# Small transfers on ScalarE's DMA queue, blocks picked by DMA reads, and new ranks in a planned mixing stage

## The chip, the cores and the metric

One Trainium2 chip, one of its cores. The metric is the device time of one execution of the kernel, in microseconds (us); of several runs the median counts. The engines of the core are TensorE (PE, with its weight loads as PEld), VectorE (DVE), ScalarE (ACT), GpSimd (POOL) and SyncE (SP). Each works through its own instructions in order; semaphores tie the engines together. A DMA is issued by an instruction on one engine (here SP, ACT or POOL) and carried out by 16 DMA engines that all issuing engines share.

## The reference

One layer of a trunk block on 1024 tokens of width 1024: RMSNorm, one projection of 9504 columns, two recurrent branches (RWKV-7 and HGRN2), a gated merge, an output projection; then cross-attention into 256 memory tokens, then a SwiGLU FFN. The change touches the RWKV-7 branch, which is, per head of width 64:

```python
def step(state, inp):
    r_t, w_t, k_t, v_t, a_t, b_t = inp
    sa = jnp.einsum('bhvk,bhk->bhv', state, a_t)
    state = (state * w_t[:, :, None, :] + sa[..., None] * b_t[:, :, None, :]
             + v_t[..., None] * k_t[:, :, None, :])
    return state, jnp.einsum('bhvk,bhk->bhv', state, r_t)
_, o = lax.scan(step, s0, (tm(r_h), tm(w_h), tm(k_mod), tm(v_h), tm(-kk), tm(kk * a_h)))
```

The kernel computes this in chunks of 64 tokens: within a chunk the delta rule is a unit triangular 64 x 64 system per head, whose inverse is built from 16 x 16 diagonal blocks, then 32 x 32, then 64 x 64.

## The kernel before

The program has three parts. `rw_prep` projects the RWKV columns and writes the branch's factors to DRAM scratch (`ar_d`, `bk_d`, `v_d`, `z_d`). `mixing` does everything up to the merged activations `y_d`. Then come output projection, attention and FFN, ordered by an automatic scheduler.

In `mixing` the order is written by a planner (`Pace`) while the program is built. Matmuls of the remaining projection (HGRN columns and gates, tile `pproj`, 768 slots of three 128x512 matmuls) are the filling; all other work is a set of generators that yield requests `on(engine, tiles, prio=...)`. `note` gives each recorded operation a planned start and duration; a request is due when its inputs, its buffer and its conditions are ready on that planned clock, and among due requests of an engine the one with the smallest `due + 2 * prio` is recorded next. PE records one such group, then three projection slots, and so on. The result is one fixed order per engine: where a transfer or an engine is later than planned, the engine waits at that instruction, with everything behind it.

RWKV work is 16 jobs (`job(n)`, 128 tokens of four pairs of heads each, so eight 64 x 64 systems for each half of the partitions). A job runs:

- SP loads AR and BK; PE forms the scores `psc`, which are masked into AR, SR and BS (BS holds the triangular systems, 64 columns each).
- The 16 x 16 diagonal blocks of BS are copied into BP by four `copy_predicated` on DVE with the mask `pk`; SP writes BP to scratch `Ad`, and SP reads `Ad` twice into Aq, so that each partition holds one 16 x 16 block.
- DVE inverts all blocks by back substitution: nine steps of a product (`pr`) and a sum (into Tq), with POOL setting the diagonal of Aq in between.
- SP writes Tq to scratch `Td` and reads it back as T1 (shown as T in the profile).
- PE, DVE and ACT grow the inverse to 32 x 32 and 64 x 64 (`py1`, `pu1`, `py2`, `pu2` in the code, py and pu in the profile; results in Yd, UD, TT, U, Y).
- The two chunks are scanned in order: `cm`, `po` matmuls with the state Z, copies R and Z by ACT, decay by DVE. Job n's scan needs job n-1's.
- Group norm and the merge terms follow on DVE, ACT and POOL (st, xc, zb), and SP writes the result to `ya_d`.

After every fourth job the results of half the tokens are complete: `merge(j, h)` reads ya_d, the spilled gates sa_d and sb_d, PE transposes (`pya`), DVE and POOL multiply and add, SP writes `y_d`. For the last column block `last_gates` does it with tiles kept on chip. The HGRN branch (`hgrn`, `state`, `level`, `blocks`; tiles poh, pyb, sc, Sh) runs in between, fed by evictions `ev_*` of the projection's PSUM tiles by ACT. At the very end of `mixing` two key tiles of the attention are projected (`pproj<-mT,wkey`, 48 matmuls), after the last transpose `pya`. Attention begins with the values (`pvv`, `values(c)`): its memory tokens mT and weights wraw use SBUF that held the projection's input uh and ul.

The requests that the change ranks anew: DVE's inversion steps (prio 0), the evictions `ev_*` (prio -1).

Of the kernel before, what the change touches and what calls it, by code (L numbers as in the profile page):

```python
# [10 lines left out]
F32 = mybir.dt.float32  # L11
F32R = mybir.dt.float32r
AF = mybir.ActivationFunctionType
# [5 lines left out]
P = 128  # L19
# [13 lines left out]
class Pace:  # L33
# [82 lines left out]
    def note(self, e, op, a, kw):  # L116
# [68 lines left out]
def tile_trunk(ctx, tc, x, mem, norm_mix_g, w_in, rw_mu, rw_w0, rw_w2, rw_a0, rw_a2, rw_g2,  # L185
# [523 lines left out]
    def unit_blocks(pk, hm, lo16, Yd):  # L709
# [3 lines left out]
        f = Yd.rearrange("p e t -> p (e t)")  # L713

        nc.gpsimd.memset(f[:, 0:64], 1.0)
        f3 = f[:, 0:64].rearrange("p (m t) -> p m t", t=16)
        for b in (0, 64):
            r = f3[b:b + 64]

            sel(out=r, in_=r, compare_op=ALU.is_gt, fill=0.0, base=0, pattern=[[16, 4], [1, 16]], channel_multiplier=-1)  # L720
            sel(out=r, in_=r, compare_op=ALU.is_ge, fill=0.0, base=0, pattern=[[-16, 4], [0, 16]], channel_multiplier=1)
        nc.gpsimd.tensor_copy(pk, f3)
# [14 lines left out]
    def mixing(mctx):  # L737
# [28 lines left out]
        pk = cp.tile([P, 4, 16], U8, name="pk")  # L766
# [3 lines left out]
        BP = cp.tile([P, 8, 16], F32, name="BP")  # L770
        Yd = cp.tile([P, 8, 32], F32, name="Yd")
        nc.gpsimd.memset(BP, 0.0)
        unit_blocks(pk, hm, lo16, Yd)
# [82 lines left out]

        def job(n):
# [65 lines left out]
            for ms in ((7, 6), (5, 4), (3, 2), (1, 0)):  # L923
                yield on("DVE", Aq, Tq)
# [9 lines left out]
            yield on("SP", Tq, prio=-1)  # L934
            Td = pace.scratch(dram, [P, 8, 16], tag="Td", bufs=2)
            nc.sync.dma_start(out=Td.rearrange("(r i g) e t -> g e r i t", r=8, g=2).rearrange("g e r i t -> (g e) (r i) t"),
                              in_=Tq.rearrange("p i t -> p (i t)"))
            yield on("SP", Td, prio=-1, room=((fp, "T1", 1),), cond=lambda: n < 1 or ("U32", n - 1) in flags)
            T1 = fp.tile([P, 8, 16], F32, tag="T1", name="T1")
            nc.sync.dma_start(out=T1, in_=Td)  # L940
# [251 lines left out]
        def ev_k(j, h, ps):  # L1192
            yield on("ACT", ps, func=AF.Sigmoid, prio=-1, cond=lambda: j == 0 or ("free", j - 1, h) in flags)
# [8 lines left out]
        def ev_q(j, h, ps):  # L1202
            yield on("ACT", ps, func=AF.Sigmoid, prio=-1, room=room("td"), cond=lambda: j == 0 or ("free", j - 1, h) in flags)
            t = TD("sgq")
            act(t, ps, AF.Sigmoid)
            yield on("DVE", t, prio=-1)
# [958 lines left out]
    n = 0  # L2165
# [181 lines left out]
```

## Time and profile before

| | us |
|---|---|
| median of 3 runs | 2354.96 (2354.55 to 2357.52) |
| profiled execution | 2350.59 |
| its span | 2348.9 |
| PE busy in the span | 2260.1 (96%) |
| DVE, ACT, POOL busy | 1578.6 (67%), 1129.5 (48%), 1028.3 (44%) |

The 1.7 us between the span and the execution's own time lie around the first and the last instruction. Matmuls are pipelined, so a busy PE is not PE at its peak; the bare time between the starts of two matmuls says more. `mixing` runs on PE from about 400 us to 1333.8 us of the span. In the profile nearly all of its instructions carry line 103, where the planner's wrapper issues them; they are told apart by tile names.

### The profile page before, as it was taken

Reading aid. Unit: us, or ns where it says so; the run is one execution under the profiler, and the core shown is the slowest. Engines: PE = TensorE matmul, PEld = TensorE weight load, DVE = VectorE, ACT = ScalarE, POOL = GpSimd, SP = SyncE. Lnnn points to the kernel's source line nnn. Section 1 sums busy time; section 2 is a strip of 40 time slices with the busy share of each in tenths; the row PEclk is TensorE's granted clock in tenths of the full one; section 3 lists DMA queues with packets and bytes.
Section 4 is the critical chain, followed back from the end, with each engine's and each line's share of the span. In section 5 each row is a group of like instructions: output and inputs, shape, how many; then the busy total and the mean of one; then the engine's idle time right before and its main releaser. Section 6 shows DMA issues by size and latency. Waiting matters only on the chain.

```text
span 2348.9 us, 46523 instructions
## 1 busy us (share of the span) xinstructions
PE 2260.1 (96%) x18006; PEld 1845.8 (79%) x18006; DVE 1578.6 (67%) x2585; ACT 1129.5 (48%) x2199; POOL 1028.3 (44%) x1100
## 2 busy tenths in 40 slices
PE   7999999999999999999997499999999999999998
PEld 5788887787888787777876488888888888888887
DVE  5888884767677777767775365655768765656665
ACT  6545554655655555456555232543453233334543
POOL 3655546656566564554653200000266565552212
PEclk9999999999999999999998699999999999999999
DMA  5444445342444343433423797225944334248653
GB/s 171 127 135 121 131 125 150 80 117 48 110 100 123 75 126 114 115 88 84 128 70 95 237 353 267 73 60 207 282 162 132 110 96 130 82 152 299 220 170 118
DMA packets 393690, 327.92 MB, mean 140 GB/s; under 512 B 107595, under 2 KB 318653, under 8 KB 392061
## 3 DMA queue, kind: packets, MB, share of 16 engines
q1 hardware_dynamic: 391549, 319.17, 45.2%
q0 software_dynamic: 1344, 4.72, 0.5%
q8 instruction: 142, 2.33, 0.4%
q10 hardware_dynamic: 576, 1.05, 0.1%
q14 instruction: 79, 0.65, 0.1%
HBM read 228.12 MB, written 96.21 MB: 138 GB/s over the span
## 4 chain that ended last, share of the span: by engine, by line
PE 73%; DVE 5%; DMA 3%; ACT 2%; issue 1%; POOL 1%; SPq 0%; POOLq 0%; DVEq 0%; ACTq 0%
PE pproj L103 21%; PE P L301 6%; PE P L302 6%; PE P L300 6%; PE acc L301 3%; PE acc L300 3%; PE acc L302 3%; PE pw L302 2%; PE pw L300 2%; PE pw L301 2%; PE cm L103 2%; PE po L103 1%; PE psc L103 1%; PE poh L103 1%; PE pq L302 1%; PE pq L301 1%
## 5 line engine op out<-in xcount | busy, mean ns | idle before, releaser
L103 PE MATMUL pproj<-uh,whi 128*128 128x512 f32 x768 | 319.4, 416 | 4.9 <-DVE q L103 4.9
L103 PE MATMUL pproj<-uh,wlo 128*128 128x512 f32 x768 | 301.1, 392 | 1.7 <-POOL wlo L103 1.7
L103 PE MATMUL pproj<-ul,whi 128*128 128x512 f32 x768 | 301.3, 392 | 0.0
L286 POOL TENSOR_TENSOR wl<-wraw,wh 128x512 fp32r<-128x512 f32 x87 | 121.9, 1408 | 200.7 <-ACT wh L282 167.7
L282 ACT ACTIVATE whi<-wraw 128x512 fp32r<-128x512 f32 (+1 forms) x166 | 100.4, 617 | 195.3 <-PE pw L302 76.6
L103 POOL TENSOR_TENSOR wlo<-wraw,whi 128x512 fp32r<-128x512 f32 x96 | 132.4, 1391 | 137.1 <-ACT whi L103 103.4
L300 PE MATMUL pproj<-uh,whi 128*128 128x512 f32 (+1 forms) x432 | 176.8, 410 | 0.9 <-ACT uh L328 0.7
L103 PEld LDWEIGHTS pproj<-uh,whi 128*128 128x128 f32 x768 | 144.3, 188 | 40.0 <-DVE q L103 6.0
L302 PE MATMUL pproj<-uh,wlo 128*128 128x512 f32 (+1 forms) x432 | 169.9, 393 | 1.8 <-POOL wlo L286 1.8
L103 PEld LDWEIGHTS pproj<-ul,whi 128*128 128x128 f32 x768 | 144.6, 188 | 32.2
L301 PE MATMUL pproj<-ul,whi 128*128 128x512 f32 (+1 forms) x432 | 169.8, 393 | 0.0
L103 PEld LDWEIGHTS pproj<-uh,wlo 128*128 128x128 f32 x768 | 145.0, 189 | 27.0 <-POOL wlo L103 2.1
L277 POOL TENSOR_TENSOR ss<-ss,nhalf 128x4 f32<-128x4 f32 (+1 forms) x7 | 6.2, 884 | 328.9 <-DMA wraw<-in_xa_wo_dram 186.6
L286 DVE TENSOR_TENSOR wlo<-wraw,whi 128x512 fp32r<-128x512 f32 x134 | 92.4, 698 | 74.6 <-ACT whi L282 72.7
L103 ACT ACT_TABLE_LOAD x100 | 128.3, 1283 | 23.1 <-PE pproj L103 11.4
L286 POOL TENSOR_TENSOR wlT<-wraw,whT 128x512 fp32r<-128x512 f32 x72 | 102.2, 1427 | 83.2 <-ACT whT L282 72.8
L282 ACT ACTIVATE wh<-wraw 128x512 fp32r<-128x512 f32 x143 | 87.1, 624 | 93.2 <-PE P L301 66.8
L301 PE MATMUL acc<-wl,th 128*128 128x512 f32 x308 | 119.9, 389 | 0.0
L300 PE MATMUL acc<-wh,th 128*128 128x512 f32 x308 | 119.8, 389 | 0.0
L302 PE MATMUL acc<-wh,tl 128*128 128x512 f32 x308 | 119.8, 389 | 0.0
L2291 DVE TENSOR_TENSOR tl<-tl,th 128x512 fp32r<-128x512 f32 x77 | 60.7, 801 | 61.1 <-ACT th L2290 60.3
L302 PE MATMUL pw<-whi,al 128*128 128x512 f32 x256 | 100.1, 391 | 1.2 <-DVE al L286 1.2
(460 smaller groups left out, 6322.1 us busy)
## 6 DMA issues: line engine op xcount, KB each, us to landing
wraw<-in_w_in_dram SPq DMA_DIRECT2D x148, 256.0 KB
wraw<-in_ffn_w_dram SPq DMA_DIRECT2D x145, 256.0 KB
y<-in_ffn_w_dram SPq DMA_DIRECT2D x22, 512.0 KB
wsum_d<-y SPq DMA_DIRECT2D x11, 1024.0 KB
hsum_d<-s SPq DMA_DIRECT2D x44, 256.0 KB
tl<-hsum_d SPq DMA_DIRECT2D x44, 256.0 KB
wraw<-wsum_d SPq DMA_DIRECT2D x44, 256.0 KB
hid_d<-s SPq DMA_DIRECT2D x33, 256.0 KB
```

The source lines that it names most:

```text
L103: r = getattr(self.engine, op)(*a, **kw)
L277: nc.gpsimd.tensor_tensor(dst, tmp, nhalf[:, 0:n], op=ALU.pow)
L282: nc.scalar.activation(hi, src, AF.Copy)
L286: e.tensor_tensor(lo, src, hi.bitcast(F32), op=ALU.subtract)
L300: nc.tensor.matmul(ps, ah, bh, start=first, stop=False)
L301: nc.tensor.matmul(ps, ah, bl, start=False, stop=False)
L302: nc.tensor.matmul(ps, al, bh, start=False, stop=last)
L2291: tt(hl, hl.bitcast(F32), hh.bitcast(F32), op=ALU.subtract)
```

## The change

Four edits, all in `mixing` and its planner:

- The six transfers of a job around the inversion (one write, two reads of Ad, Td, T1) are issued by ACT instead of SP; the write of Ad is now two DMAs, one for each half of the partitions.
- BP, `pk` and the four predicated copies are gone. The whole of BS goes to DRAM (64 columns per row instead of 16), and the two reads of Aq pick the diagonal blocks, 16 runs of 16 floats for each of 64 partitions, by an access pattern with a pitch of 16 x 64 + 16. Since what is below and on the blocks' diagonals now arrives too, DVE multiplies Aq by a mask `tri` once per job.
- Ranks: the inversion's DVE steps go from prio 0 to -1, the projection's evictions from -1 to -2.
- The planner takes an ACT transfer to be independent of SP's queue, and to land 2.0 us plus its bytes by rate after its start.

```diff
         if op == "dma_start":
-            start = max(start, self.landings[-8], self.read.get(aps[0].name, 0.0))
+            start = max(start, self.landings[-8] if e == "SP" else 0.0, self.read.get(aps[0].name, 0.0))
...
-            took = 0.5
-            self.dma = max(start + 0.9, self.dma) + 4 * math.prod(aps[0].shape) / rate
-            self.landings.append(self.dma + 1.1)
-            late = self.landings[-1] - start - took
+            took = 0.62
+            if e == "ACT":
+                late = 2.0 + 4 * math.prod(aps[0].shape) / rate - took
+            else:
+                self.dma = max(start + 0.9, self.dma) + 4 * math.prod(aps[0].shape) / rate
+                self.landings.append(self.dma + 1.1)
+                late = self.landings[-1] - start - took
...
-    def unit_blocks(pk, hm, lo16, Yd):
+    def unit_blocks(tri, hm, lo16, Yd):
...
+        nc.gpsimd.memset(tri, 1.0)
+        sel(out=tri, in_=tri, compare_op=ALU.is_gt, fill=0.0, base=0, pattern=[[-1, 16], [1, 16]], channel_multiplier=0)
...
+        DIAG = 16 * 64 + 16
+        def blocks16(d):
+            rows = d.rearrange("e h (b y) -> (e h b) y", y=DIAG)[:, 0:16 * 64]
+            return rows.rearrange("r (s t) -> r s t", t=64)[:, :, 0:16]
...
-            yield on("DVE", BS, over=(BP,), cond=lambda: n < 1 or ("Ad", n - 1) in flags)
-            for b in range(4):
-                nc.vector.copy_predicated(BP, pk[:, b, :].unsqueeze(1).to_broadcast([P, 8, 16]),
-                                          BS[:, :, 16 * b:16 * b + 16])
-            Ad = pace.scratch(dram, [64, 16, 16], tag="Ad", bufs=2)
-            yield on("SP", BP, prio=-1)
-            nc.sync.dma_start(out=Ad.rearrange("(e r) s t -> (r s) e t", r=8), in_=BP)
+            yield on("ACT", BS, prio=-1)
+            Ad = pace.scratch(dram, [8, 2, 4 * DIAG], tag="Ad", bufs=2)
+            for hh in range(2):
+                nc.scalar.dma_start(out=Ad[:, hh, 0:64 * 64].rearrange("e (s t) -> s e t", t=64), in_=BS[H[hh]])
...
-            yield on("SP", Ad, prio=-1, room=((fp, "Aq", 1), (fp, "Tq", 1)), cond=lambda: n < 1 or ("inv", n - 1) in flags)
+            yield on("ACT", Ad, prio=-1, room=((fp, "Aq", 1), (fp, "Tq", 1)), cond=lambda: n < 1 or ("inv", n - 1) in flags)
...
-                nc.sync.dma_start(out=Aq[64 * g:64 * g + 64], in_=Ad)
+                nc.scalar.dma_start(out=Aq[64 * g:64 * g + 64], in_=blocks16(Ad))
...
-            yield on("DVE", Aq, Tq)
+            yield on("DVE", Aq, Tq, prio=-1)
...
+            nc.vector.tensor_tensor(Aq, Aq, tri, op=ALU.mult)
...
-                yield on("DVE", Aq, Tq)
+                yield on("DVE", Aq, Tq, prio=-1)
...
-            yield on("SP", Tq, prio=-1)
+            yield on("ACT", Tq, prio=-1)
...
-            nc.sync.dma_start(out=T1, in_=Td)
+            nc.scalar.dma_start(out=T1, in_=Td)
...
-            yield on("ACT", ps, func=AF.Sigmoid, prio=-1, cond=lambda: j == 0 or ("free", j - 1, h) in flags)
+            yield on("ACT", ps, func=AF.Sigmoid, prio=-2, cond=lambda: j == 0 or ("free", j - 1, h) in flags)
```

The last pair stands for all evictions (`ev_k`, `ev_q`, `ev_s`, `ev_g`, `ev`, `ev_sa`), on DVE too.

Since the planner decides the order, the program's order shows what moves. Before `mixing` nothing does, on any engine, and PE's instructions behind `mixing` stand as before. First place, PE at the end of `mixing`. Before, behind the last projection matmul (which stands just ahead of these rows) come job 15's two scan steps (cm, po), the end of the HGRN branch (psA to poh, pyb), five transposes and the keys:

```order
L103 MATMUL cm<-Z,AR_3701 64x64 x8
L103 MATMUL po<-Z,AR_3701 64x64 x8
L103 MATMUL psA<-m_15512 32x32 x8
L103 MATMUL psl<-m_15534 64x64 x8
L103 MATMUL poh<-iv,sc 64x128 x8
L103 MATMUL poh<-Sh,qe 64x128 x8
L103 MATMUL cm<-R,U 64x64 x8
L103 MATMUL cm<-Z,BKT 64x64 x8
L103 MATMUL po<-Z,SR 64x64 x8
L103 MATMUL cm<-Z,AR_3701 64x64 x8
L103 MATMUL po<-Z,AR_3701 64x64 x8
L103 MATMUL cm<-R,U 64x64 x8
```

Now PE has only this behind its last projection matmuls (first row), up to the first value matmul of the attention:

```order
L103 MATMUL pproj<-ul,whi 128x512
L103 MATMUL pya<-ident,mya 128x128 x4
L103 MATMUL pproj<-mT,wkey 128x256 x48
L303 MATMUL pvv<-whi,mT 128x512
L304 MATMUL pvv<-wlo,mT 128x512
```

Everything else has moved ahead of the last projection matmul. Second place, PE where job 15's last scan matmul (po<-Z,SR) now stands:

```order
L103 MATMUL pproj<-ul,whi 128x512
L103 MATMUL po<-Z,SR 64x64 x8
L103 MATMUL poh<-iv,sc 64x128 x8
L103 MATMUL poh<-Sh,qe 64x128 x8
L103 MATMUL pproj<-uh,whi 128x512
L103 MATMUL pproj<-uh,wlo 128x512
```

Behind it stand 246 projection matmuls, where there were none before. Counted in projection slots, a job's way from its last score to its py1 falls from 52 to 38 on average over the 16 jobs. Third place, ACT around job 15's Td, which SP issued before:

```order
L103 ACTIVATE sgs<-pproj 128x512
L103 ACTIVATE whi<-wraw 128x512
L103 ACTIVATE sgg<-pproj 128x512
L103 ACTIVATE Y<-py_14268 32x256
L103 DMA Td<-Tq 16x64x16
L103 ACTIVATE U<-pu_14303 32x8x32 x2
L103 ACTIVATE R<-cm 128x256
L103 DMA T_14370<-Td 128x128
L103 ACTIVATE Z<-cm 64x4x64 x2
```

The transfers of job 15 now stand among job 14's scan copies (R, Z), evictions (sgs, sgg) and weight splits (whi).

More of the change, by code (lines that the diff above doesn't have):

```diff
@@ L763, in mixing @@
             nc.gpsimd.memset(U[64 * hh + 32:64 * hh + 64, :, 0:32], 0.0)
-        pk = cp.tile([P, 4, 16], U8, name="pk")
+        tri = cp.tile([P, 16, 16], F32, name="tri")
         hm = cp.tile([P, 2, 16], F32, name="hm")
         lo16 = cp.tile([P, 16], U8, name="lo16")
-        BP = cp.tile([P, 8, 16], F32, name="BP")
         Yd = cp.tile([P, 8, 32], F32, name="Yd")
-        nc.gpsimd.memset(BP, 0.0)
-        unit_blocks(pk, hm, lo16, Yd)
+        unit_blocks(tri, hm, lo16, Yd)
         cm = pc.tile([P, 2, 4, 64], F32, name="cm")
@@ L1202, in ev_q @@
         def ev_q(j, h, ps):
-            yield on("ACT", ps, func=AF.Sigmoid, prio=-1, room=room("td"), cond=lambda: j == 0 or ("free", j - 1, h) in flags)
+            yield on("ACT", ps, func=AF.Sigmoid, prio=-2, room=room("td"), cond=lambda: j == 0 or ("free", j - 1, h) in flags)
             t = TD("sgq")
             act(t, ps, AF.Sigmoid)
-            yield on("DVE", t, prio=-1)
+            yield on("DVE", t, prio=-2)
             q = X[j]["q", h] = B2("q")
@@ L1212, in ev_s @@
         def ev_s(j, h, ps):
-            yield on("ACT", ps, func=AF.Sigmoid, prio=-1, room=room("td"), cond=lambda: j == 0 or ("out", j - 1, h) in flags)
+            yield on("ACT", ps, func=AF.Sigmoid, prio=-2, room=room("td"), cond=lambda: j == 0 or ("out", j - 1, h) in flags)
             t = TD("sgs")
             act(t, ps, AF.Sigmoid)
-            yield on("DVE", t, prio=-1)
+            yield on("DVE", t, prio=-2)
             s = X[j]["sb", h] = pace.hold(B2("sb"))
@@ L1221, in ev_g @@
         def ev_g(j, h, ps):
-            yield on("ACT", ps, func=AF.Sigmoid, prio=-1, room=room("td"))
+            yield on("ACT", ps, func=AF.Sigmoid, prio=-2, room=room("td"))
             t, s = TD("sgg"), X[j]["sb", h]
@@ L1232, in f @@
             def f(j, h, ps):
-                yield on("ACT", ps, prio=-1, room=room("td"))
+                yield on("ACT", ps, prio=-2, room=room("td"))
                 t = X[j][name, h] = TD(name)
@@ L1270, in ev_sa @@
             if j == NU - 1:
-                yield on("ACT", ps, func=AF.Sigmoid, prio=-1, room=room("td"))
+                yield on("ACT", ps, func=AF.Sigmoid, prio=-2, room=room("td"))
                 t = TD("sa")
@@ L1281, in ev_sa @@
             nc.sync.dma_start(out=g, in_=gd[j, h])
-            yield on("ACT", ps, func=AF.Sigmoid, prio=-1)
+            yield on("ACT", ps, func=AF.Sigmoid, prio=-2)
             act(t, ps, AF.Sigmoid)
```

12 lines of the change are left out of this document (2 added, 10 removed).

## The prediction

> **What bounds the kernel now.** I read the page's busy shares first, then the 40 slices, then the windows of the stages, then PE's timeline in the one stage that stands out.
>
> ```profile
> span 2348.9 us, 46523 instructions
> PE 2260.1 (96%) x18006; PEld 1845.8 (79%) x18006; DVE 1578.6 (67%) x2585; ACT 1129.5 (48%) x2199; POOL 1028.3 (44%) x1100
> PE   7999999999999999999997499999999999999998
> PEclk9999999999999999999998699999999999999999
> ```
>
> PE is busy nearly throughout, so a faster DVE or a shorter transfer is worth nothing unless PE waits for it. The slices show one hole, the 22nd and 23rd (7, then 4), and there the granted clock falls too (8, 6). In numbers, each window's columns being its length, busy us of PE, PEld, DVE, ACT, POOL, then PE's clock, DMA share and GB/s:
>
> ```profile
> 400.00:1267.50 867.50, 850.57 (x11316) 684.01 (x11315) 623.59 (x1278) 494.17 (x1070) 497.23 (x544) 1.00 0.37 94
> 1267.50:1333.80 66.30, 24.30 (x282) 21.41 (x282) 17.95 (x31) 14.06 (x42) 17.16 (x16) 0.61 0.69 225
> 1333.80:1465.00 131.20, 127.42 (x628) 107.57 (x627) 75.15 (x121) 44.72 (x80) 2.10 (x3) 1.00 0.85 301
> ```
>
> The first row is `mixing` up to its last projection matmul: PE idles 17 us in 867. The second is from there to the attention's first value matmul: 66.3 us with 24.3 us of work, most of it at half clock. The hole in PE's own words, start and duration, with the idle time before it in brackets:
>
> ```profile
> 1266.95 0.39 PE L103 MATMUL pproj<-uh,wlo 128*128 128x512 f32 x1
> 1267.18 0.39 PE L103 MATMUL pproj<-ul,whi 128*128 128x512 f32 x1
> 1267.49 0.69 PE L103 MATMUL cm<-Z,AR 128*64 128x64 f32 x16
> 1275.98 1.12 PE L103 MATMUL cm<-Z,AR 128*64 128x64 f32 x16 [1.05 <-DVE Z L103]
> 1285.46 1.52 PE L103 MATMUL po<-Z,SR 128*64 128x64 f32 x16 [4.37 <-ACT Z L103]
> 1306.73 2.83 PE L103 MATMUL pya<-ident,mya 128*128 128x128 f32 x12 [19.75 <-DMA mya<-ya_d]
> 1325.08 1.08 PE L103 MATMUL pya<-ident,mya 128*128 128x128 f32 x4 [6.29 <-DMA mya<-ya_d]
> 1333.76 0.39 PE L300 MATMUL pvv<-whi,mT 128*128 128x512 f32 x1
> ```
>
> The filling has run out at 1267.5, but job 15 has only begun its scan (cm). Its scan, its group norm, its write to ya_d and the merges that read it back are a chain with nothing beside it: its three waits for mya alone are 34.2 us (the group's row stands in the sum below). So the RWKV jobs' latency, harmless while projection matmuls fill in, sets the end of `mixing`.
>
> Why is job 15 late? Its transfers and its inversion:
>
> ```profile
> 1211.89 0.37 SPq L103 DMA_DIRECT2D Ad<-BP  x1
> 1215.30 1.20 SPq L103 DMA_DIRECT2D Aq<-Ad  x2
> 1221.68 0.28 DVE L103 TENSOR_TENSOR pr<-Aq 128x128 f32<-128x128 f32 x1
> 1239.17 0.42 DVE L103 TENSOR_REDUCE Tq<-pr 128x16 f32<-128x256 f32 x1
> 1239.62 0.56 SPq L103 DMA_DIRECT2D Td<-Tq  x1
> 1242.22 0.34 SPq L103 DMA_DIRECT2D T<-Td  x1
> ```
>
> From BP's write to T's read it is 30.3 us, of which 17.9 are the inversion's sixteen DVE products and sums plus its first two steps, with other DVE work placed between them at equal or better rank. The transfers themselves are short: Td landed 2.6 us after its issue.
>
> **The change, part by part.** *The predicated copies go, a mask comes.*
>
> ```profile
> L103 DVE COPY_PREDICATED BP<-pk,BS 128x128 f32<-128x128 uint8 x64 | 45.1, 705 | 1.7
> 1264.59 0.43 DVE L103 TENSOR_TENSOR m<-m,k 128x256 f32<-128x256 f32 x1 [2.39 <-ACT m L103]
> ```
>
> DVE loses 45.1 us and gains 16 products of 128x256, each 0.43 by the row of that shape: 6.9. DVE was busy 623.6 of 867.5 us, so the net 38 us come off an engine that does not bound the stage. Directly they are worth nothing; per job they take some 2.4 us out of the chain.
>
> *The transfers go to ACT.* Six issues per job, 96 in all. Issues of these tiles held SP 0.34 to 0.60 us each; ACT's own first issue in this trace is like that:
>
> ```profile
> 1274.97 0.39 ACTq L1704 DMA_DIRECT2D wraw<-in_xa_wv_dram  x1
> ```
>
> At 0.5 us it is 48 us more on ACT, from 494.2 to 542 of 867.5 us (62%). That is covered as long as ACT is not what PE waits for. Beside the issue there is a wait: ACT stands at Aq's read until Ad has landed, and at T's read until Td has. Ahead of T's read the order has three copies (U twice, R) behind Td's issue, and behind it Z, for which PE waits. So a late landing that SP took at no cost now holds R, Z and the evictions. Per wait between 0 (the planner has put it where it is over) and 2.6 us (the landing row above, nothing between), 32 times: 0 to 83 us of ACT, of which PE sees what its order has no slack for.
>
> *Blocks picked by reads.* Ad's write has 1024 runs as before, of 256 B instead of 64; the reads of Aq have 2048 runs of 64 B instead of 128 of 1 KB. Td's write, 1024 runs of 64 B, is the nearest row. The window in which it ran almost alone:
>
> ```profile
> 1239.60:1242.30 2.70, 2.70 (x25) 1.98 (x23) 1.74 (x5) 2.65 (x5) 1.99 (x3) 1.00 0.23 24
> ```
>
> A share of 0.23 of 16 engines over 2.7 us is 9.9 engine-us, so 9.7 ns a run; 2048 runs are 1.2 us over 16 engines. Bounds for what a job's T loses by it: nothing (the two reads overlap in flight) to 2.6 us (a second Td on top). I take 1.2, less than the 2.4 us that the copies give back.
>
> *Ranks.* Inversion first takes the waiting out of 17.9 us on DVE; evictions first take it out of PE's waits for PSUM. No edit has a price on PE by itself. What counts is the order that comes out: job 15's last scan matmul now has 246 projection matmuls behind it, and only one transpose and the keys stand behind the last of these. At 0.23 us from start to start (1266.95 to 1267.18) the 246 are 57 us of cover. The chain behind that matmul was 1285.46 to 1325.08, 40 us, and had DMA traffic for the attention in its way. It fits.
>
> **The sum**, against the profiled execution's 2350.59 us (1.7 outside the span).
>
> - The stretch 1267.5 to 1333.8 goes: -66.3.
> - Its work stays, at full clock. The groups:
>
> ```profile
> L103 PE MATMUL pproj<-mT,wkey 128*128 128x256 f32 x48 | 8.1, 345 | 0.0
> L103 PE MATMUL pya<-ident,mya 128*128 128x128 f32 x20 | 5.0, 426 | 34.2 <-DMA mya<-ya_d 34.2
> 1243.10 0.66 PE L103 MATMUL pkh<-ident,kh 128*128 128x128 f32 x4
> 1344.80 0.28 PE L301 MATMUL pk<-mT,whi 128*128 128x256 f32 x1
> 1344.92 0.28 PE L302 MATMUL pk<-mT,wlo 128*128 128x256 f32 x1
> ```
>
>   Five transposes at 0.66 (pkh, same shape) are 3.3 instead of 5.0; 48 key matmuls at 0.12 from start to start (pk, same shape) 5.8 instead of 8.1; of the other 11.2 us about half ran slow (cm 1.12 instead of 0.69), which leaves about 8.6. Together +17.7, of which 6.5 (one transpose, keys) stand behind the last projection matmul.
> - Late next is the attention's start, since its weights and mT use SBUF of uh and ul and cannot be loaded while projections read these. Before, the same loads, issued by ACT at 1274.97, became usable here:
>
> ```profile
> 1282.58 0.63 ACT L282 ACTIVATE whi<-wraw 128x512 fp32r<-128x512 f32 x1 [3.70 <-DMA wraw<-in_xa_wv_dram]
> 1283.24 0.69 DVE L286 TENSOR_TENSOR wlo<-wraw,whi 128x512 fp32r<-128x512 f32 x1 [5.22 <-ACT whi L282]
> ```
>
>   That is 9.0 us from the issue to the end of wlo, and the issue comes about 0.5 us after the last projection matmul. So the first value matmul can start 9.5 us after it, of which 6.5 are covered: +3.0 (0 to 8, the upper end if mT, which ended up in the same burst, comes last).
> - Behind that, what the attention had loaded during the hole must be loaded beside its work. It eats a weight tile of 256 KB in six matmuls, 1.4 us or 187 GB/s, and the third window row shows 301 GB/s moved; but other loads share these, and that row lost 3.8 us to waits. I take the like of it once more: +3 (0 to 12).
> - `mixing` itself, whose PE order is now denser: the first window row lost 17 us in 16 jobs. Between -10 (evictions first removes waits for PSUM) and +83 (every landing wait of ACT reaches PE) I stay near that row, a third more: +5.
>
> -66.3 + 17.7 + 3.0 + 3 + 5 = -37.6, or 2313.0 on the profiled execution's level. The median of the runs, 2354.96, lies 4.4 above that execution; on its level **2317 us**. The forecast's own range is 2299 (mixing -10, no gap, no refill loss) to 2331.
>
> **The rivals.** *ACT pays.* If each of the 32 landing waits costs PE 1 us instead of 32 waits costing 5 together, that is +27: 2344. For it: the order has T's read three copies behind Td's issue, 1.1 us of work for a landing of 2.6, at 0.38 for a copy:
>
> ```profile
> 1258.80 0.38 ACT L103 ACTIVATE U<-pu 32x256 f32<-32x256 f32 x1 [0.48 <-DVE U L103]
> ```
>
> Against it: the planner places the read where it expects the landing, and ACT keeps 38% of the stage free.
>
> *PE waits at py1, slower.* PE's order is fixed and py1 now stands 38 slots behind a job's last score instead of 52. A slot is 867.5 / 768 = 1.13 us, so T has to be there 16 us sooner. Sure of that are 2.4 us from the copies and what the rank takes out of the 17.9. If T is late by 4 us in each job, PE waits 64 us instead of 5: 2376. It turns slower than before when the lateness passes (37.6 + 5) / 16 = 2.7 us a job. For it: 2048 short runs per job, and ACT in line for everything. Against it: Td's 2.6 us, and a case where the old queue itself was the delay:
>
> ```profile
> 832.83 0.37 SPq L103 DMA_DIRECT2D Ad<-BP  x1
> 833.29 2.58 SPq L103 DMA_DIRECT2D Z<-v_d  x4
> 835.96 0.55 SPq L103 DMA_DIRECT2D sa_d<-sa  x1
> 836.61 2.56 SPq L103 DMA_DIRECT2D AR<-ar_d  x4
> 839.26 0.56 SPq L103 DMA_DIRECT2D BK<-bk_d  x1
> 839.87 0.51 SPq L103 DMA_DIRECT2D zb<-z_d  x1
> 840.43 1.60 SPq L103 DMA_DIRECT2D Aq<-Ad  x2
> ```
>
> Here 7.6 us passed against 3.4 for job 15, with eleven other transfers issued by SP in between. The Trainium skill, "DMA: Bandwidth & Descriptors", section "Issuing engines are not separate DMA queues", says that DMAs from all issuing engines run on the same 16 DMA engines, so that a second one saves the issuing time alone. By that rule a landing gets no shorter, which is this rival's case; the two rows agree in that the 4.2 us between them are other issues, not a longer landing.
>
> *The attention starves.* Gap 8 and refill 12 instead of 3 and 3: +14, 2331. For it: the DMA share of 0.85 in the third row. The Trainium skill, "TensorE: Matmul & The Clock Gate", part 1, has the clock halve after an idle window of about 3.4 us; by it the gap of 3 costs no clock and one of 8 costs about 2 us more (an estimate from that page). The hole above agrees, with a clock of 0.61.
>
> *The hole stays.* If the merges remain a chain (pya from 1306.73 to 1326.2, 19.5 us) whatever the jobs do, 20 us of the gain are gone: 2337. Against it stand the orders: four of five transposes have moved in front.
>
> **How the numbers follow.** Forecast 0.60, ACT pays 0.17, attention starves 0.11, hole stays 0.04, PE waits at py1 0.08. Measurement tells about 0.2%, 4.7 us, from no change. Only the last case is slower; the upper end of "ACT pays" touches no change, 0.04. Faster 0.88, same 0.04, slower 0.08. The range: 2299 from the forecast's lower end, 2344 as the price of "ACT pays", which leaves out the slower case and the tails.
>
> **What would show it.** Right: the slices lose their hole and half clock; the wait of pya for mya falls from 34.2 us to a few; job 15's last po stands some 60 us or more ahead of the last projection matmul; the window from the last projection matmul to the first pvv is 9 to 15 us instead of 66; from inversion's first to last DVE row under 12 us instead of 17.9; ACT's busy share in `mixing` unchanged (issues aren't counted) but waits for Ad and Td by name. Wrong: PE idle in `mixing` over 45 us, with py waiting for T (PE waits), or cm and py waiting for ACT's Z, R, U (ACT pays); or over 10 us idle in the first 130 us of the attention.

## The result, and the profile after

Four runs of the changed kernel: 2314.25 to 2322.77 us, median **2317.44**; of the kernel before beside them 2353.94 to 2357.52, median 2354.76. The ratio is 0.9842, 95% interval 0.982 to 0.9864: 37 us faster. The profiled execution is the slowest of the four (2322.77, span 2321.1), 5.3 us above the median, where the profiled one of before lay 4.4 below the median that the forecast was set on. So from profile to profile only 27.8 us are gone, and the terms below add up to that.

The page of the changed kernel, span, busy shares and slices:

```profile
span 2321.1 us, 46517 instructions
PE 2266.5 (98%) x18006; PEld 1845.9 (80%) x18006; DVE 1528.3 (66%) x2510; ACT 1134.9 (49%) x2214; POOL 1027.7 (44%) x1109
PE   7999999999999999999999999999999999999998
PEclk9999999999999999999999999999999999999999
```

The hole in the 22nd and 23rd slice is gone, with its half clock. The stages, in windows with the same columns as before (length, busy us of PE, PEld, DVE, ACT, POOL, clock, DMA share, GB/s): `mixing` to the end of its last projection matmul, from there to the first value matmul, the next 131 us, and all that is behind that value matmul:

```profile
400.00:1291.50 891.50, 869.46 (x11560) 697.84 (x11559) 586.56 (x1224) 510.11 (x1120) 513.88 (x567) 0.99 0.42 104
1291.50:1298.96 7.46, 6.46 (x53) 6.21 (x52) 1.73 (x4) 1.23 (x2) 3.15 (x3) 1.00 0.96 316
1298.96:1430.26 131.30, 128.11 (x620) 106.27 (x621) 79.27 (x128) 46.07 (x83) 2.66 (x4) 1.00 0.93 332
1298.96:2321.10 1022.14, 1007.56 (x4644) 834.24 (x4644) 646.70 (x935) 409.39 (x761) 306.39 (x228) 0.99 0.53 176
```

The stretch of 66.3 us is 7.5 now, with one us of it idle. PE's own rows (start, duration, idle time ahead in brackets) of job 15's last scan step, of the last projection matmul and of what follows it:

```profile
1209.40 0.69 PE L103 MATMUL po<-Z,SR 128*64 128x64 f32 x16
...
1291.19 0.39 PE L103 MATMUL pproj<-ul,whi 128*128 128x512 f32 x1
1292.26 0.63 PE L103 MATMUL pya<-ident,mya 128*128 128x128 f32 x4 [0.68 <-DMA mya<-ya_d]
1292.64 6.00 PE L103 MATMUL pproj<-mT,wkey 128*128 128x256 f32 x48
1298.96 0.50 PE L303 MATMUL pvv<-whi,mT 128*128 128x512 f32 x1 [0.32 <-ACT whi L285]
```

Job 15's scan now ends 82 us ahead of the last projection matmul. The chain behind it (norm, ya_d, merges) runs beside projections, and of pya's 34.2 us of waiting 0.7 is left at the end. But did job 15's inversion get faster? Its transfers and the first and last DVE row of the inversion:

```profile
1137.63 0.62 ACTq L103 DMA_DIRECT2D Ad<-BS  x1
1141.56 1.33 ACTq L103 DMA_DIRECT2D Aq<-Ad  x2
1146.87 0.29 DVE L103 TENSOR_TENSOR pr<-Aq 128x128 f32<-128x128 f32 x1
1158.80 0.42 DVE L103 TENSOR_REDUCE Tq<-pr 128x16 f32<-128x256 f32 x1
1160.39 0.57 ACTq L103 DMA_DIRECT2D Td<-Tq  x1
1164.69 0.34 ACTq L103 DMA_DIRECT2D T<-Td  x1
```

From Ad's write to the end of T's issue it is 27.4 us; before it was 30.7 (1211.89 to 1242.56). Three us shorter, and 74 us earlier: the job moved, it hardly shrank. Over all 16 jobs the same stretch is 34.3 us on average, 37.6 before. What moved it is what the experiments are about.

### The profile page after: what moved, and what is told of

Its sections match the earlier page's. It is cut to its first block, busy times and chain, and to the rows that moved or that the text cites. A ratio compares the mean times of both kernels' runs of the same rounds, so it can differ in the third digit from the quotient of the medians.

```text
span 2321.1 us, 46517 instructions
## 1 busy us (share of the span) xinstructions
PE 2266.5 (98%) x18006; PEld 1845.9 (80%) x18006; DVE 1528.3 (66%) x2510; ACT 1134.9 (49%) x2214; POOL 1027.7 (44%) x1109
## 4 chain that ended last, share of the span: by engine, by line
PE 69%; DMA 5%; DVE 4%; POOL 3%; issue 2%; ACT 2%; SPq 0%; ACTq 0%; POOLq 0%; DVEq 0%
PE pproj L103 19%; PE P L304 6%; PE P L303 6%; PE P L305 6%; PE acc L304 3%; PE acc L305 2%; PE acc L303 2%; PE cm L103 2%; PE pw L305 2%; PE pw L303 2%; PE pw L304 2%; PE poh L103 1%; PE pq L304 1%; PE pq L303 1%; PE pq L305 1%
## 5 line engine op out<-in xcount | busy, mean ns | idle before, releaser
L103 PEld LDWEIGHTS pproj<-uh,wlo 128*128 128x128 f32 x768 | 145.8, 190 | 24.9
L303 PE MATMUL pw<-whi,ah 128*128 128x512 f32 x256 | 100.6, 393 | 0.6 <-ACT ah L285 0.6
```

What stands on the lines that cost most here:

```text
L103: r = getattr(self.engine, op)(*a, **kw)
L303: nc.tensor.matmul(ps, ah, bh, start=first, stop=False)
```

## The experiments

Each result is the median in us, in brackets the lowest and the highest run, and the ratio to the kernel before, run beside it, with its 95% interval. In all of them, "slot" counts the 768 groups of three projection matmuls in PE's order, 1.13 us each, and says how many of them stand ahead of job 15's last `po`: 768 before, 686 in the changed kernel. The theory (A in the expectations): the time is set by how much projection work the order leaves behind that `po`. The first rival (B, C): what the edits do on the chip, faster transfers by ACT, no copies, inversion first, is what brings T earlier.

### Each part alone, and the plan without the queue

The kernel before with the transfers on ACT and the planner's new account of them:

```diff
-            yield on("SP", BP, prio=-1)
-            nc.sync.dma_start(out=Ad..., in_=BP)
+            yield on("ACT", BP, prio=-1)
+            nc.scalar.dma_start(out=Ad..., in_=BP)
...
```

(So for Aq, Td and T1 too; the planner's account as in the change.)

> The kernel before with one part of the change: the six transfers of a job go by ACT, and the planner takes them to be independent of SP and to land 2.0 us plus bytes after their start. Predicated copies, the compact Ad and the old ranks stay. Job 15's last scan matmul (po) stands behind slot 676 of 768 of the projection (before 768, changed kernel 686). Theory A (the time is that of the changed kernel plus whatever of the 37 us of the hole has no projection slots behind job 15's last po, 1.13 us a slot): 92 slots are 104 us of cover, so no hole, 2317, within 0.3%. Rival B (the picks by reads or the ranks carry it, as they shorten the job itself): 2340 to 2355, with a hole left. If the 2 us per job of the copies count on PE: 16 x 2 = 32 more, 2349.

Measured: **2301.9** (2299.65 to 2304.04), ratio 0.9771 (0.9751 to 0.9791). No hole, as A says, but 15 us below the changed kernel and below A's 2317, which neither side expected.

The kernel before with the new ranks alone:

```diff
-            yield on("DVE", Aq, Tq)
+            yield on("DVE", Aq, Tq, prio=-1)
-            yield on("ACT", ps, func=AF.Sigmoid, prio=-1, ...)
+            yield on("ACT", ps, func=AF.Sigmoid, prio=-2, ...)
```

> The kernel before with the new ranks alone (inversion before the evictions' old rank, evictions first). Job 15's last po stands behind slot 762 of 768. Theory A: 6 slots x 1.13 are 7 us of cover, so 7 of the 37 us go: 2348 (2340 to 2355). Rival B (ranks carry the gain, since the inversion's 17.9 us shrink to under 12 and PE waits less for PSUM): 2317 to 2330.

Measured: **2336.3** (2335.46 to 2338.3), ratio 0.992 (0.9897 to 0.9943). Between the two ranges. The hole stays (52.3 us from the last projection matmul to the first value matmul, 36.9 of them idle instead of 42.0), and the order happens to wait less inside `mixing` (6.8 us idle instead of 16.9). So the ranks by themselves give 18 us under the old account. Of the 36.9 us, 13.5 are `pyb` waiting for `yn`, the end of the HGRN branch: job 15's chain is not the only late one, and A counts that one alone.

The changed kernel with the transfers on SP and the account as before:

```diff
-            yield on("ACT", BS, prio=-1)
+            yield on("SP", BS, prio=-1)
-                nc.scalar.dma_start(out=Ad[...], in_=BS[H[hh]])
+                nc.sync.dma_start(out=Ad[...], in_=BS[H[hh]])
...
```

(So for Aq, Td and T1 too.)

> The changed kernel with the six transfers back on SP and the planner's old account of them; picks by reads, mask, one write of Ad as two DMAs and the new ranks stay. Job 15's last po stands behind slot 768 of 768. Theory A: no cover, the whole hole, 2355 (2348 to 2362). Rival B (picks and ranks shorten the job on the chip, whatever the order): 2330 or less.

Measured: **2348.0** (2347.2 to 2351.53), ratio 0.9973 (0.9963 to 0.9983). Picks and ranks by themselves give 6 us; the hole is whole (69.5 us), and the time is at the lower edge of A's range.

The same, but with the new account for these transfers though SP issues them:

```diff
+            quick = aps[0].name.split("_")[0] in ("Ad", "Aq", "Td", "T1", "T")
-            start = max(start, self.landings[-8], self.read.get(aps[0].name, 0.0))
+            start = max(start, self.landings[-8] if not quick else 0.0, self.read.get(aps[0].name, 0.0))
...
+            if quick:
+                late = 2.0 + 4 * math.prod(aps[0].shape) / rate - took
```

> As the kernel before it in this list (all transfers issued by SP, picks, new ranks), but the planner is told the changed kernel's account for the six transfers: out of SP's line of landings, 2.0 us plus bytes. Only the plan changes, not the queue. Job 15's last po stands behind slot 672, the last transpose behind 750. Theory A with a fast enough SP: 2315 (2308 to 2322), no waits of py for T. Rival C (ACT's queue is physically needed, since behind SP's other issues a job's transfers pass 7.6 us instead of 3.4 as at 832.83 in the trace before): each job's T is late by about 4 us or more, PE waits for T at py, 16 x 4 = 64 us or more: 2380, and the profile names py<-T or the inversion behind Aq.

Measured: **2301.3** (2298.9 to 2303.14), ratio 0.9768 (0.9748 to 0.9788), and no row of PE in its profile names T as what it waited for. Rival C fell: SP delivers in time. A's range (2308 to 2322) was missed too, by 7 us on the fast side.

### The plan alone, and everything but the plan

That left one suspect. The kernel before with the account alone (the last diff, on the kernel before). No line that does the kernel's work changes. The planner decides more than the order, though: on its clock it also chooses ACT or DVE for a copy and DVE or POOL for some products (`copy` and `either` in the kernel). So PE's 18006 matmuls and all DMAs stay on their engines, while DVE has 2564 instructions instead of 2585, ACT 2207 instead of 2199 and POOL 1107 instead of 1100; the expectation's "each engine gets the instructions of the kernel before" is not quite so.

> The kernel before with one part of the change alone, the planner's account of the six transfers (apart from SP's line, landing 2.0 us plus bytes). They stay on SP, the predicated copies and the old ranks stay: each engine gets the instructions of the kernel before, in another order. Job 15's last po stands behind slot 677 of 768, all transposes in front of slot 759. Theory A' (the order is all; the instructions that the change adds and removes are worth nothing by themselves): 2302, like the kernels with the queue alone and with the account alone (2301.9 and 2301.3). Rival C (something on the chip is needed, the copies gone or ACT's queue, for T to land in time): PE waits at py or U for it, at least 1 us a job, 2318 or more.

Measured: **2309.2** (2306.56 to 2310.2), ratio 0.9808 (0.9791 to 0.9824). That is 7 us above A' and 9 below C; PE waits 0.6 us in all for T, far from C's 1 us a job. And the opposite, the changed kernel with all its instructions and the old account:

```diff
-            start = max(start, self.landings[-8] if e == "SP" else 0.0, self.read.get(aps[0].name, 0.0))
+            start = max(start, self.landings[-8], self.read.get(aps[0].name, 0.0))
...
-            if e == "ACT":
-                late = 2.0 + 4 * math.prod(aps[0].shape) / rate - took
```

> The changed kernel with all its instructions (ACT's queue, picks, mask, new ranks) under the planner's old account of transfers. Last po behind slot 768. Theory A': the hole is back, 2345 to 2358, as in the kernel with SP, picks and ranks (2348.0). Rival C (the edits on the chip shorten a job's chain in fact): the hole is shorter by what they save and the time is 2335 or less.

Measured: **2348.0** (2346.89 to 2348.76), ratio 0.9974 (0.9963 to 0.9985), as A' says. The windows of the account alone (`mixing` to its last projection matmul, then to the first value matmul), and job 15's transfers there:

```profile
400.00:1282.38 882.38, 867.15 (x11554) 695.04 (x11553) 613.50 (x1275) 500.10 (x1109) 515.95 (x565) 0.99 0.40 102
1282.38:1293.31 10.93, 7.88 (x54) 7.55 (x52) 3.63 (x8) 3.00 (x9) 2.63 (x3) 0.84 0.90 322
```

```profile
1129.01 0.37 SPq L103 DMA_DIRECT2D Ad<-BP  x1
1155.08 0.34 SPq L103 DMA_DIRECT2D T<-Td  x1
```

The same two windows of the changed instructions under the old account:

```profile
400.00:1256.69 856.69, 852.47 (x11154) 681.49 (x11153) 573.83 (x1200) 499.63 (x1070) 496.76 (x556) 1.00 0.40 99
1256.69:1328.87 72.18, 25.71 (x441) 22.61 (x441) 20.91 (x36) 15.43 (x52) 20.92 (x18) 0.60 0.62 207
```

With SP, the copies and the old ranks, but the new account, 46 us go. With ACT, picks, mask and new ranks, but the old account, 7 go, and the hole is 72 us long. So **the gain is that of the account**: 2.0 us and bytes, out of SP's line, in place of a line in which each transfer waits for the one ahead. In the planner of the kernel before the reads of Aq land 4.6 to 12.4 us after their start, with the new account 3.3; these are the plan's numbers, not the chip's. Which part of the account does it (out of the line, the 2.0 us, or the 0.62 us for an issue) no run separates, and how much of the 46 us is the order and how much the other choice of engines isn't separated either. A late landing in the plan makes the planner place everything behind it later in the fixed order, and the chip then works through that order, whether the data was there long ago or not. From Ad's write to the end of T's issue a job takes, over all 16 on the chip, 37.6 us before, 27.4 with the account alone, 42.1 with all edits under the old account.

### A truer account

If the account is what counts, is a truer one better? The reads of Aq landed 5.3 to 8.0 us after the first issue, in the six jobs of the changed kernel where DVE waited for them; the plan has 3.3. The number is one for all four tiles, however: Td, for which this plan has 5.3 as well, landed 2.6 us after its issue on the chip (the prediction's row of before; 2.6 is the shortest in the changed kernel too). So the account below is truer for Aq and further off for Td.

```diff
-                late = 2.0 + 4 * math.prod(aps[0].shape) / rate - took
+                late = 4.0 + 4 * math.prod(aps[0].shape) / rate - took
```

> The changed kernel with one number changed: the account has ACT's transfers land 4.0 us plus bytes after their start instead of 2.0, so 5.3 for the reads of Aq, nearer to the 5.3 to 8.0 that the trace of the changed kernel shows. Last po behind slot 743, last transposes behind 768. Theory A': 25 slots x 1.13 are 28 us of cover for a chain that cost 47 to 52 (2348 to 2354 against 2302), so 20 us of it are left: 2322 to 2326, if DVE's wait at Aq gets shorter and mixing's idle goes from 22 to about 10 us; 2335 if it doesn't. Rival F (an account that is true to the landing is the better plan): 2310 or less.

Measured: **2336.1** (2329.16 to 2338.35), ratio 0.9916 (0.9899 to 0.9932). DVE's wait at Aq fell from 18.0 to 1.8 us, as the later number should do, and idle in `mixing` from 22.0 to 13.1; but the hole came back: 42.8 us from the last projection matmul to the first value matmul, 24.9 of them idle. It is slower than A's 2322 to 2326, since A took the chain behind `po` as a constant: here the last po starts at 1251.88 and the last pya at 1307.36, 55 us, where before it was 40.

### Where the last 15 us are

Two kernels without a hole take 2301.3 and 2301.9, the changed one 2317.4. The same windows of the kernel with the queue alone:

```profile
400.00:1274.47 874.47, 863.80 (x11543) 693.47 (x11541) 619.71 (x1285) 501.49 (x1113) 505.44 (x557) 1.00 0.40 102
1274.47:1280.76 6.29, 6.29 (x53) 6.25 (x53) 1.09 (x3) 1.23 (x2) 1.29 (x1) 1.00 0.89 303
```

From profile to profile the changed kernel is 20.0 us longer (its profiled execution is its slowest), 17.0 of them in `mixing`: 22.0 us of idle against 10.7, and the rest is half clock. PE's longest waits in the changed kernel, and windows laid over what follows them:

```profile
427.85 1.09 PE L103 MATMUL pkh<-ident,kh 128*128 128x128 f32 x4 [4.86 <-DVE kh L103]
...
500.17 0.49 PE L103 MATMUL pproj<-ul,whi 128*128 128x512 f32 x1 [1.81 <-issue]
```

```profile
427.50:432.50 5.00, 4.65 (x13) 3.90 (x14) 4.73 (x12) 1.88 (x4) 4.10 (x4) 0.51 0.58 141
500.00:507.50 7.50, 7.33 (x56) 5.64 (x56) 3.27 (x10) 3.54 (x18) 0.00 (x0) 0.55 0.23 73
```

Behind a wait of 1.81 us PE is busy for 7.3 us at a clock of 0.55. Busy time times what the clock lacks to 1, summed over windows of 2.5 us, is 8.7 us lost in `mixing` of the changed kernel, 3.2 with the queue alone, 1.7 before. So 11.3 of idle and 5.5 of clock make up 16.8 of the 17.0.

The copies back in the changed kernel, in place of picks and mask:

```diff
-            nc.vector.tensor_tensor(Aq, Aq, tri, op=ALU.mult)
+            for b in range(4):
+                nc.vector.copy_predicated(BP, pk[:, b, :]..., BS[:, :, 16 * b:16 * b + 16])
```

> The changed kernel with the predicated copies and the compact Ad in place of the picks by reads and the mask; queue, account and new ranks stay. Last po behind slot 682. Theory D (the 15 us by which the changed kernel is behind the kernel with the queue alone come from the picks, whose reads land 5.3 to 8.0 us after their issue there where the plan has 3.3, so that DVE stands 18.0 us at Aq with PE's inputs behind it): 2302. Rival E (they come from the ranks, or from the luck of one order): 2310 to 2320.

Measured: **2311.1** (2307.41 to 2311.94), ratio 0.9812 (0.9797 to 0.9826). As E says, with 9 us left between it and the kernel with the queue alone, to which it only adds the ranks. Then the plan of the changed kernel kept to the letter (PE, DVE, ACT and POOL go through `mixing` with the same instructions in the same order), with SP issuing the transfers:

```diff
+        def by_sp(**kw):
+            nc.sync.engine.dma_start(**kw)
+            pace.note("ACT", "dma_start", (), kw)
-                nc.scalar.dma_start(out=Ad[...], in_=BS[H[hh]])
+                by_sp(out=Ad[...], in_=BS[H[hh]])
```

> The changed kernel with its plan untouched: PE, DVE, POOL and ACT work through mixing in the changed kernel's order, only that the six transfers of a job, at their places in the program, are issued by SP instead of ACT. Theory D' (the changed kernel's 15 us more than the kernel with the account alone on SP, 2317 against 2301, come from ACT's issues and landing waits, and from picks that land 5.3 to 8.0 us after an issue by ACT where they took 3.7 to 5.1 by SP): 2300 to 2306, DVE's wait at Aq down from 18.0 us to under 8. Rival E (they are the short waits of this one order, each with a stretch of half clock behind it): 2313 to 2320, with the 4.9 us wait of pkh for kh still there.

Measured: **2309.0** (2307.22 to 2316.56), ratio 0.9811 (0.9791 to 0.9831). Neither side's number. The same pair of rows in the trace of the changed kernel (issue of the reads, then DVE's first use with its wait):

```profile
1057.54 1.33 ACTq L103 DMA_DIRECT2D Aq<-Ad  x2
1065.58 0.43 DVE L103 TENSOR_TENSOR Aq<-Aq,tri 128x256 f32<-128x256 f32 x1 [6.05 <-DMA Aq<-Ad]
```

and by SP, in the same place of the order:

```profile
1047.57 1.30 SPq L851 DMA_DIRECT2D Aq<-Ad  x2
1052.27 0.81 DVE L103 TENSOR_TENSOR Aq<-Aq,tri 128x256 f32<-128x256 f32 x1 [2.34 <-DMA Aq<-Ad]
```

8.0 us by ACT, 4.7 by SP; over all waits 5.3 to 8.0 (six) against 3.6 to 5.2 (eight). In the three other orders of the changed kernel below, ACT's took 3.4 to 7.9 (16 waits), so the queue is not all that sets it. Yet DVE's wait at Aq only went from 18.0 to 17.1 us, so D' is wrong in its mechanism: what went are the 1.81 us wait with its half clock, and three of 1.3 to 1.5 us for ACT's Z, R and sa; one of 2.1 us for ACT's Y came instead. The wait of pkh for kh stays at 5.0. In medians ACT's queue costs 8 us here; the two intervals overlap, so this is likely and not firm.

The changed kernel without its ranks, and with jobs planned every 40 or 42 slots instead of 41:

```diff
-            yield on("DVE", Aq, Tq, prio=-1)
+            yield on("DVE", Aq, Tq)
-            yield on("ACT", ps, func=AF.Sigmoid, prio=-2, ...)
+            yield on("ACT", ps, func=AF.Sigmoid, prio=-1, ...)
```

```diff
-        PERIOD = 41
+        PERIOD = 40
```

> The changed kernel with the old ranks (inversion 0, evictions -1); queue, account and picks stay. Last po behind slot 712 of 768, the last transposes behind 766 and 768. Cover of 56 slots, 63 us, so no hole to speak of. Theory G (ranks cost, as the pair 2301.9 without and 2311.1 with them says for the kernels with copies): 2305 to 2309. Theory H (picks cost, as 2317.4 against 2311.1 says): 2307 to 2311 too, but with DVE's wait at Aq as long as in the changed kernel, 12 to 18 us. Rival E (order's luck): anywhere from 2301 to 2318.

> The changed kernel with jobs planned to start every 40 slots instead of 41: the same instructions in another order, last po behind slot 699, last transposes behind 762 and 768. Rival E (hole-free orders of one set of instructions differ by 10 us or more through their short waits): differs from 2317.4 by over 4.7 us either way. Theory D/G/H (the instructions and ranks set the 15 us): 2314 to 2321.

> As the run before it, with jobs every 42 slots: last po behind slot 708, last transposes behind 763 and 768. Rival E: 2301 to 2320 and not the same as with 40 or 41. Theory D/G/H: 2314 to 2321.

Measured: without ranks **2317.4** (ratio 0.9842, 0.9828 to 0.9857), with 40 slots **2320.0** (0.9846, 0.9827 to 0.9864), with 42 slots **2308.3** (0.9804, 0.9789 to 0.9819). Without ranks PE waited 4.0 us for yn, and then the last transpose 8.0 us for mya: its chain from po (1221.33) to pya (1288.26) took 67 us, so 63 us of cover were not enough, against G and H both. With 40 slots E missed its own condition (2.6 us from 2317.4, not over 4.7) and the range of D, G and H held; with 42 it was the other way round. The step from 40 to 42 slots, with the same work in the program, moves the time by 11.7 us.

These three are not free of a hole. Behind the last projection matmul PE idles 12.0, 6.3 and 3.6 us, against 1.0 in the changed kernel, and first of all for the end of the HGRN branch, with 40 slots and with 42:

```profile
1302.64 1.11 PE L103 MATMUL pyb<-ident,yn 128*128 128x128 f32 x4 [6.26 <-DVE yn L103]
```

```profile
1274.92 1.11 PE L103 MATMUL pyb<-ident,yn 128*128 128x128 f32 x4 [3.58 <-DVE yn L103]
```

So the cover behind `po` is not the whole story, and among the kernels with the new account the slots do not rank the times. From 40 to 42 slots `mixing` is 17.1 us shorter in the profiles and this stretch 2.5, but what lies behind the first value matmul, where PE's work is the same, is 8.6 longer; over all fourteen profiles that part takes 1011.5 to 1023.5 us. The pairs that differ by single edits disagree as well. The ranks cost 9 us on top of the queue alone (2301.9 to 2311.1) and nothing in the changed kernel (2317.4 both ways), and under the old account they gain 18. Picks and mask cost 6 us with ACT's queue (2311.1 to 2317.4), while picks and ranks together gain 8 with SP's (2309.2 to 2301.3). So orders of the same work differ by nearly as much as the 15 us in question, and no single edit of the change can be charged with them.

The idle column is PE's idle time from the last projection matmul to the first value matmul, in each kernel's profile.

| kernel | account | issued by | slots | idle | us |
|---|---|---|---|---|---|
| before | old | SP | 768 | 42.0 | 2354.8 |
| all edits, old account | old | ACT | 768 | 46.5 | 2348.0 |
| picks and ranks | old | SP | 768 | 42.6 | 2348.0 |
| ranks | old | SP | 762 | 36.9 | 2336.3 |
| account landing 4.0 | between | ACT | 743 | 24.9 | 2336.1 |
| changed, 40, 41, 42 slots | new | ACT | 699, 686, 708 | 6.3, 1.0, 3.6 | 2320.0, 2317.4, 2308.3 |
| changed, old ranks | new | ACT | 712 | 12.0 | 2317.4 |
| changed, copies | new | ACT | 682 | 1.0 | 2311.1 |
| account alone | new | SP | 677 | 3.1 | 2309.2 |
| changed, order kept | new | SP | 686 | 1.0 | 2309.0 |
| queue alone | new | ACT | 676 | 0.0 | 2301.9 |
| account, picks and ranks | new | SP | 672 | 0.2 | 2301.3 |

Every kernel with the new account is below every one with an older one. The last two beat both kernels of this study, by 52 us against before and 15 to 16 against the changed one.

## Why the prediction came out

The time was met, and the mechanism that carries it (the chain of job 15 moves under the projections, the hole goes) is what the trace shows. That it was met to the microsecond is luck of the level: the sum, made against the profiled execution, said -37.6, and from profile to profile it is -27.8. The 9.8 us between them are made good by chance, since one profile lay 4.4 below its median and the other 5.3 above. One sum is wrong: -10 for `mixing`, no gap and no refill loss are 21 us under 2317, so the lower end of the range is 2296 and not 2299.

- *The stretch goes, its work stays* (-66.3 and +17.7): right; one transpose and the keys stand behind the last projection matmul.
- *The attention's start* (+3.0): +1.0, the window of 7.5 us less the 6.5 covered. The 9.5 us, taken from loads in the hole of before, were too many, and the window is shorter than the 9 to 15 us named as a sign. Of the 9.5, the 0.5 from the last projection matmul to ACT's first load had no row behind it; it came out at 0.4 (1291.19 to 1291.61).
- *Behind that* (+3): +7.0, 1022.1 us from the first value matmul against 1015.1 before. PE is busy 5.0 us more there (1007.6 against 1002.6 in the same stretch of before) and idle 2.0 more. Of the 5.0, 3.0 are half clock (the same sum over windows; none there before), behind a wait of 2.41 us at 1712.78. The first 131 us idle 3.2, well under the 10 that "starves" would need. No run isolates the cause.
- *Mixing* (+5): **mis-sized**, +12.8 (891.5 against 867.5 and the 11.2 us of work that moved in). The idle part was right almost to the digit, 22.0 against 17, but by a guess: 4.9 of it is pkh's wait for kh, which the prediction did not name, and ACT's Z, R and sa, its reason for more waits, make 4.2. What lacked is the clock: 8.7 us lost to stretches of half clock against 1.7, which the sum had put only on the hole.
- *Job 15's last po 60 us or more ahead*: 82. *pya's wait a few us*: 0.7. *Inversion under 12 us*: just missed, 1146.87 to 1159.22 is 12.4 instead of 17.9.
- *Blocks picked by reads* (1.2 us more, bounds 0 to 2.6): open. By ACT the picks landed 5.3 to 8.0 us after their issue, and the compact reads by ACT, in the kernel with the queue alone, took 3.5 to 5.5 in its three waits. But in the changed kernel with copies the compact reads took 2.8 to 6.3 by ACT, and by SP they took 2.8 to 5.4 (account alone) where picks took 3.6 to 5.2. The ranges overlap, so the form of the reads alone does not set the landing. DVE, with the inversion in front, stood 18.0 us at Aq in six jobs, which the prediction did not see.
- *ACT pays* (+27): about +8, by the kernel that keeps the order and lets SP issue, and not firm, since the intervals overlap. The landing waits by name are there, 9.4 us on ACT for Td in four rows; PE's waits for ACT's Z, R and sa are 4.2.
- *PE waits at py1*: no such wait in the changed kernel. The concern was that T must come 16 us sooner while only the copies and the ranks give anything for sure. It assumed that the old order had T just in time. It had not: the same SP transfers fit an order with `po` at slot 677.

The step that failed is the **attribution**. The prediction said that no edit has a price by itself and that "what counts is the order that comes out", but it looked for the cause of the order in copies, ranks and the queue, and took the 7.6 us at 832.83 as a sign that SP's queue was the delay. The runs put the gain on the fourth edit, the account, which the prediction costed nowhere: 46 us with it alone, 7 with the three others without it. On the rule quoted there, the Trainium skill, "DMA: Bandwidth & Descriptors", section "Issuing engines are not separate DMA queues", the trace agrees: by ACT's queue the landing got no shorter (8.0 us against SP's 4.7 in the pair above), and the gain did not need it.

## What to carry to other kernels

Where a planner fixes the order, a change of its estimates is an edit like any other, and often the largest: test it alone, with the work left as it is, and test the other edits without it. See what else the planner decides by its clock; here it also moved copies and products between engines. An estimate that is too late costs the end of the stage, because the order then holds work back that is ready; one that is too early cost less here (with 4.0 instead of 2.0 idle in `mixing` fell by 9 us, and the time rose by 19). And when several edits come with a new order, differences of 10 us between orders with little or no hole are no verdict on an edit until orders of the same work have been compared.

## What the runs showed of the hardware

**Half clock after short waits.** A wait of 1.81 us was followed by 7.5 us at a clock of 0.55, one of 1.35 us (pproj for sa, at 855.49) by 5 us at 0.64 and 0.68, while one of 1.50 us (cm for Z, at 915.56) had none. The Trainium skill, "TensorE: Matmul & The Clock Gate", part 1, has the clock halve after an idle window of about 3.4 us; here less than that did, so the measurement decides, and a short wait can cost more than its own length again: behind the 1.81 us, 7.33 us of work at 0.55 lost 3.3 us.

**DVE behind POOL.** The inversion's first product took 1.41 us in the first job, where a product of POOL had begun just ahead of it, and 0.29 in job 15 (row above), where POOL ran none. In another job POOL's product began just behind it, and it took 0.29 again:

```profile
422.48 1.27 POOL L103 TENSOR_TENSOR qe<-q,eb 128x512 f32<-128x512 f32 x1
422.49 1.41 DVE L103 TENSOR_TENSOR pr<-Aq 128x128 f32<-128x128 f32 x1
...
425.95 1.75 DVE L103 TENSOR_TENSOR kh<-kh,k 128x512 f32<-128x512 f32 x1
```

```profile
562.61 0.29 DVE L103 TENSOR_TENSOR pr<-Aq 128x128 f32<-128x128 f32 x1
```

```profile
562.63 1.42 POOL L103 TENSOR_TENSOR wlo<-wraw,whi 128x512 fp32r<-128x512 f32 x1 [0.94 <-ACT whi L103]
```

Over the 16 jobs of the changed kernel it is 1.26 to 1.41 in the three with POOL's product ahead, 0.29 in the two with it just behind and in the eleven without one.

In the first job such slowed products, with kh behind them, fill the 4.86 us for which PE waited at 427.85, and that wait, 4.3 to 5.3 us, is in the profiles of all four kernels with the new account, the picks and ACT's queue, and not in that with SP's queue, picks and its own order, where pkh waits for nothing. No run took it away and left the rest, so what it costs with its clock, some 7 us by the rows (4.86 and 4.65 times 0.49), is an estimate.
